# x laid out by features, and 1 / rms(x) moved from the rows of x to the results of the projections

## The chip, the cores and the metric

The kernel runs on one core of a Trainium2 chip. A core has a matrix engine, TensorE (PE in the profile; PEld is its loading of weights), VectorE (DVE), ScalarE (ACT), GpSimd (POOL) and SyncE (SP), which here only issues transfers (DMAs). Each engine executes its own list of instructions in order and waits on semaphores for the others. The metric is the device time of one execution in microseconds (us); of several runs the median counts.

## What is computed

One layer of a streaming encoder on 1024 prompt frames and 64 sample frames of width 1024, 1088 rows in all:

```python
h = rmsnorm(x, g_mix)                       # x * rsqrt(mean(x*x) + eps) * g_mix
[q_a,k_a,v_a | q_b,k_b,v_b | f_b | gate] = h @ w_in
A = band attention(q_a, k_a, v_a)           # 8 heads, QK norm, learned bias
B = forgetting attention(q_b, k_b, v_b)     # 8 heads, c = cumsum of log sigmoid(f + b_f)
x = x + (sigmoid(gate_a) * (A @ w_pa) + sigmoid(gate_b) * (B @ w_pb)) @ w_o
x = x + HierMoE(rmsnorm(x))                 # 32 experts, top-1 group, then top-2 in it
```

Since 1 / rms(x) is one number for each frame, `(x / rms) @ W` equals `(x @ W) / rms`; g_mix is multiplied into the rows of w_in.

## The kernel before

All products that must be exact to fp32 are made of three faster ones: an operand is split into a rounded high part and the rest (`w` hi and lo, `hTh` and `hTl`), and hi*hi, hi*lo and lo*hi are summed in PSUM. Frames stand in nine tiles, eight of 128 prompt frames and tile 8 of the 64 sample frames, taken in the order `TILES` = 0, 1, 2, 3, 4, 5, 8, 6, 7.

`load_x` starts the program: it loads x by frames (128 frames by 1024 features, 512 KB a tile), a few constants, and the weights of the first pair of heads. A frame tile is scaled by 1 / rms (`norm_first` for tile 0, `norm_h` for the others: a square with sum on ACT, two small steps on DVE and POOL, then a multiply of 128x1024 on DVE) and turned: `turn_h` makes eight transposes on PE (L95, 128x128 each), four to a PSUM buffer; ACT copies them to `hTh` (L193) and DVE writes the rest to `hTl` (L194).

`qkv(x)` projects q, k and v of one of eight pairs of heads, x = 0 to 3 of branch A and 4 to 7 of branch B: for every frame tile 24 matmuls of 384 columns (392 for the pair that also carries the forget gates; 16 for tile 8, whose high and low parts stand side by side in one operand). Only `qkv(0)` has the transposes of the next tile between its matmuls, and it is the one that works up all nine frame tiles. ACT copies the result to `raw` (L380), `normalize` and `normalize2` make the QK norm on ACT, DVE and POOL, and `turn_qk` transposes q and k. In the last tile of a pair the weights of the next are split (`load_hi` on ACT, L227; `load_lo` on DVE, L234).

`attention` runs pair by pair, its steps put between the matmuls of later projections, and after the last pair between those of the gates: `gate(ab, c, dst)` computes one of 2 x 8 blocks of 128 gate columns in three slices of 384, 384 and 320 frames, and ACT writes tanh(z / 2) of each to SBUF straight from PSUM (L751). When the prompt's attention of branch B has ended, `swap(1)` frees its memory and starts `sample` for the eight pairs of the sample frames, one every 24 steps. `merge(0)`, the other gates of branch B, and `merge(1)` follow, then `out` (w_o, router) and the experts.

PE's order is the program's order, written with two counters (`at`: steps, one for three matmuls; `late`: modelled PE time). For the other engines and SP a scheduler orders the instructions from a modelled time line, except in the first stage (`self.first`), in which ACT and DVE follow the program too.

## Time and profile before

| | us |
|---|---|
| median of 3 runs (lowest 1236.16, highest 1239.33) | 1238.21 |
| the profiled execution | 1233.42 |
| its span, from the first to the last instruction | 1231.6 |
| PE busy in the span | 1175.8 |
| DVE, ACT, POOL busy | 800.6, 740.5, 317.7 |

The profiled execution is 1.82 us longer than its span and 4.79 us below the median. PE is busy almost throughout: the three stretches with less are the first 10 us, the sample frames' attention around 610 to 700 us, and the experts at the end, where the DMA engines are near full.

### The profile page before, as it was taken

To read this page: it belongs to the slowest core of one execution; us is meant where nothing else is said; L and a number is where in the kernel's file an instruction comes from. 1 tells how busy PE (TensorE), PEld (TensorE's weight loads), DVE (VectorE), ACT (ScalarE), POOL (GpSimd) and SP (SyncE) were. 2 spreads that over 40 slices of the span, in tenths; PEclk is the share of its full clock that TensorE was granted. 3 is DMA by queue.
4 is the path that set the end of the run, shared out by engine and by line. 5 is a ranking of instruction groups with operands and counts; after the bars stand their busy time and mean duration, and the time that the engine had idled before them with its cause. 6 is when DMAs were issued, how large, how long until landed. Compare 5 with 4: busy or idle time off the path is not lost. (4 is left out here: it accounts for less than half of the span.)

```text
span 1231.6 us, 22308 instructions
## 1 busy us (share of the span) xinstructions
PE 1175.8 (95%) x7605; PEld 1098.2 (89%) x7605; DVE 800.6 (65%) x2476; ACT 740.5 (60%) x1730; POOL 317.7 (26%) x469
## 2 busy tenths in 40 slices
PE   8999999999999999999999899999999979999983
PEld 6899999999889999899899899999988859999972
DVE  6768776767498897978467686218644444665553
ACT  5789998989498898988566344323233322333321
POOL 2643435353433444100000000000000013455421
PEclk9999999999999999999999999999999998999998
DMA  8112121222323140411234332214574458999994
GB/s 285 53 58 88 37 73 53 67 70 66 74 70 69 51 87 30 83 56 40 66 94 120 100 92 84 80 45 129 205 282 167 154 191 258 282 280 263 269 276 112
DMA packets 102539, 152.65 MB, mean 124 GB/s; under 512 B 14477, under 2 KB 78837, under 8 KB 102389
## 3 DMA queue, kind: packets, MB, share of 16 engines
q1 hardware_dynamic: 92789, 124.43, 33.6%
q0 software_dynamic: 7168, 17.84, 6.4%
q10 hardware_dynamic: 2464, 8.91, 1.8%
q8 instruction: 61, 1.00, 0.3%
q14 instruction: 57, 0.47, 0.1%
HBM read 122.08 MB, written 38.23 MB: 130 GB/s over the span
## 5 line engine op out<-in xcount | busy, mean ns | idle before, releaser
L83 PE MATMUL big<-w,hTh 128*128 128x384 f32 (+1 forms) x1152 | 322.9, 351 | 1.1 <-ACT raw L380 0.4
L83 PEld LDWEIGHTS big<-w,hTh 128*128 128x128 f32 x1152 | 203.9, 189 | 6.5 <-ACT w L227 1.1
L83 PE MATMUL big<-hTh,w 128*128 128x384 f32 (+1 forms) x768 | 204.0, 334 | 0.0
L83 PE MATMUL big<-w,hTl 128*128 128x384 f32 (+1 forms) x512 | 172.9, 338 | 1.3 <-DVE hTl L194 1.3
L83 PEld LDWEIGHTS big<-hTh,w 128*128 128x128 f32 x768 | 137.7, 188 | 1.2
L83 PE MATMUL big<-hTl,w 128*128 128x384 f32 (+1 forms) x384 | 126.0, 328 | 0.0
L636 DVE TENSOR_TENSOR PT<-small,PT 128x512 fp32r<-128x512 f32 (+2 forms) x192 | 98.7, 519 | 16.5 <-ACT PT L635 15.0
L536 ACT ACTIVATE S<-S,mns 128x640 f32<-128x640 f32 (+7 forms) x128 | 94.1, 735 | 23.7 <-DVE mns L598 22.4
L83 PE MATMUL big<-ath,w 128*128 128x384 f32 (+1 forms) x384 | 99.4, 335 | 0.0
L540 ACT ACTIVATE S<-S,rc 128x640 f32<-128x640 f32 (+7 forms) x128 | 93.8, 736 | 8.2 <-DVE rc L538 7.3
L83 PEld LDWEIGHTS big<-w,hTl 128*128 128x128 f32 x512 | 96.6, 189 | 1.8 <-DVE hTl L194 1.6
L95 PE MATMUL small<-ident,S 128*128 128x128 f32 x528 | 89.4, 274 | 3.4 <-ACT S L540 2.9
L635 ACT CAST PT<-small 128x512 fp32r<-128x512 f32 (+2 forms) x192 | 84.5, 447 | 11.2 <-PE small L83 4.7
L83 PE MATMUL small<-PT,v 128*128 128x256 f32 x608 | 83.6, 283 | 0.0
L83 PEld LDWEIGHTS small<-PT,v 128*128 128x128 f32 x608 | 79.5, 189 | 0.5 <-DVE PT L636 0.2
L411 POOL TENSOR_TENSOR ssr<-ssa,mhalf 128x8 f32<-128x8 f32 (+1 forms) x40 | 61.2, 1530 | 69.2 <-DVE ssa L410 58.4
L95 PEld LDWEIGHTS small<-ident,S 128*128 128x128 f32 x528 | 66.2, 140 | 11.5 <-ACT S L540 5.0
L83 PE MATMUL big<-wo,mh 128*128 128x512 f32 x288 | 75.9, 402 | 0.0
L83 PEld LDWEIGHTS big<-hTl,w 128*128 128x128 f32 x384 | 72.4, 189 | 0.1
L83 PEld LDWEIGHTS big<-ath,w 128*128 128x128 f32 x384 | 69.0, 190 | 1.4
L83 PE MATMUL big<-k,qh 128*128 128x320 f32 (+3 forms) x192 | 65.2, 343 | 4.7 <-DVE mns L598 4.4
L449 POOL TENSOR_TENSOR v<-raw,v 128x128 fp32r<-128x128 f32 x64 | 33.3, 521 | 134.5 <-DVE v L448 127.6
(259 smaller groups left out, 2554.9 us busy)
## 6 DMA issues: line engine op xcount, KB each, us to landing
uo<-in_w SPq DMA_DIRECT2D x43, 512.0 KB, 8.2
ux<-in_w SPq DMA_DIRECT2D x30, 512.0 KB, 7.6
ur<-in_w SPq DMA_DIRECT2D x23, 512.0 KB, 7.6
wraw<-in_w_pair SPq DMA_DIRECT2D x56, 192.0 KB, 2.8
wraw<-in_w_in SPq DMA_DIRECT2D x32, 192.0 KB, 2.5
atd<-at SPq DMA_DIRECT2D x32, 128.0 KB, 1.7
bias<-ccd SPq DMA_DIRECT2D x8, 512.0 KB, 9.1
y<-in_x_prompt SPq DMA_DIRECT2D x8, 512.0 KB, 4.3
```

What stands on the lines that cost most here:

```text
L83: self.nc.tensor.matmul(out, a, b, start=start, stop=stop)
L95: self.nc.tensor.transpose(out, a, ident)
L411: nc.gpsimd.tensor_tensor(r[:n, :4 * c], a[:n, :4 * c], self.mhalf[:n, :4 * c], op=OP.pow)
L449: (nc.gpsimd if V_POOL & 2 else nc.vector).tensor_tensor(V[:, i, :, 64:128], src, V[:, i, :, 0:64].bitcast(F32), op=OP.subtract)
L536: nc.scalar.activation(S[:nq, :n], S[:nq, :n], AF.Exp, bias=mn[:nq], scale=-1.0, accum_out=sm[:nq])
L540: nc.scalar.activation(S[:nq, :n], S[:nq, :n], AF.Copy, scale=rc[:nq])
L635: nc.scalar.copy(hi, pt[:, sr, :])
L636: nc.vector.tensor_tensor(PT[:, 1, sr, 128 * j:128 * j + 128], pt[:, sr, :], hi.bitcast(F32), op=OP.subtract)
```

## The change

x comes in laid out by features as well (`x_t`, `x_ts`, made on the host), so that the transposes go: `split_x` copies a whole tile of 128 features x 8 x 128 frames to `hTh` on ACT and subtracts on DVE. x by frames is still loaded, behind it, for the sum of squares alone (`norm_x`); 1 / rms stands in `self.r`, one column for a tile. The copies from PSUM to `raw` multiply by it. For the gates it is needed along the frames: it goes out to DRAM with the transposed `cc`, and in `swap(1)` one DMA brings it to all 128 partitions (`rb`, 128x1088). Gate results are copied plainly from PSUM; `squash` then multiplies by `rb` on POOL and takes tanh on ACT. Slices that were done before `swap(1)` wait in `bare`. Before the sample's memory is freed, `keep_r` copies `rb` to three of the four small PSUM buffers, and the later gates of branch B multiply on DVE from there. Some sample buffers (`qh`, `sat`, `sbot`) go from two to one, the two copies of cached rows (`rolled`) are asked for 60 steps later, and the warm-up matmuls use `tribig` in place of the removed `identb`.

```diff
     def load_x(self):
-        self.xs = [self.xp.tile([128, D], F32, name=f"x{i}") for i in range(NT)]
-        for hf in range(2):
-            sl = slice(512 * hf, 512 * hf + 512)
-            nc.sync.dma_start(self.xs[0][:, sl], self.x_rows(0)[:, sl])
+        self.xt[0] = self.xp.tile([128, 8, 128], F32, name="xt", bufs=5)
+        nc.sync.dma_start(self.xt[0][:, 0:2], I["x_t"][0][:, 0:2])
         self.late_consts()
-        self.norm_first()
...
+        self.load_hi(0, 0)
+        nc.sync.dma_start(self.xt[0][:, 2:4], I["x_t"][0][:, 2:4])
+        self.split_x(0, 0, 2)
+        self.load_lo(0, 0)
+        self.load_hi(0, 1)
+        self.split_x(0, 2, 4)
+        self.load_lo(0, 1)
...
+        nc.sync.dma_start(self.xt[0][:, 4:8], I["x_t"][0][:, 4:8])
+        self.split_x(0, 4, 8)
...
+        for o, i in enumerate(TILES):
+            if o:
+                self.xt[i] = self.xp.tile([128, 8, 128], F32, name="xt", bufs=5)[:, :, :rows(i)]
+                nc.sync.dma_start(self.xt[i], I["x_t"][i] if i < 8 else I["x_ts"])
+            if o:
+                self.load_rows(TILES[o - 1])
...
+    def split_x(self, i, k0, k1):
+        nc, n = self.nc, rows(i)
+        h, l = (x[:, k0:k1, 128 * i:128 * i + n] for x in (self.hTh, self.hTl))
+        x = self.xt[i][:, k0:k1]
+        nc.scalar.copy(h, x)
+        nc.vector.tensor_tensor(l, x, h.bitcast(F32), op=OP.subtract)
...
+    def norm_x(self, i):
+        nc, x = self.nc, self.xs[i]
+        jk = self.xp.tile([128, D], BF, name="jk")
+        ss = self.sp.tile([128, 1], F32, name="ssx")
+        nc.scalar.activation(jk, x, AF.Square, accum_out=ss)
+        nc.vector.tensor_scalar(ss, ss, 1.0 / D, EPS, op0=OP.mult, op1=OP.add)
+        nc.gpsimd.tensor_tensor(self.r[:, i:i + 1], ss, self.mhalf[:, 0:1], op=OP.pow)
...
     def qkv(self, x):
-                    self.at(H_TURN, self.turn_h, TILES[o + 1], 0)
-                    self.at(H_TURN + 1, self.turn_h, TILES[o + 1], 4)
...
+            if x == 0 and 0 < o < NT - 1:
+                self.split_x(TILES[o + 1], 0, 8)
+            if x == 0 and o:
+                self.norm_x(i)
...
-                nc.scalar.copy(raw[:, i % 2], ps[:, :384])
+                nc.scalar.activation(raw[:, i % 2], ps[:, :384], AF.Copy, scale=self.r[:, i:i + 1])
...
     def gate(self, ab, c, dst):
-            nc.scalar.activation(dst[:, s0:s0 + sn], ps[:, :sn], AF.Tanh, scale=0.5)
+            nc.scalar.copy(dst[:, s0:s0 + sn], ps[:, :sn])
+            if self.rb:
+                self.squash(dst, s0, sn)
+            else:
+                self.bare.append((dst, s0, sn))
+    def squash(self, dst, s0, sn):
+        nc, d = self.nc, dst[:, s0:s0 + sn]
+        if len(self.rb) == 3:
+            nc.vector.tensor_tensor(d, d, self.rb[s0 // 384][:, :sn], op=OP.mult)
+        else:
+            nc.gpsimd.tensor_tensor(d, d, self.rb[0][:, s0:s0 + sn], op=OP.mult)
+        nc.scalar.activation(d, d, AF.Tanh, scale=0.5)
+    def load_r(self, pool):
+        rb = pool.tile([128, NTOK], F32, name="rb", bufs=1)
+        self.nc.sync.dma_start(rb, self.rd.partition_broadcast(128))
+        self.rb = [rb]
+    def keep_r(self):
+        ps = [self.pp.tile([128, 384], F32, name="small", bufs=NSMALL) for _ in SL]
+        for (s0, sn), x in zip(SL, ps):
+            self.nc.scalar.copy(x[:, :sn], self.rb[0][:, s0:s0 + sn])
+        self.rb = ps
...
         def swap(br):
-            for x, pr in enumerate(pairs):
+            self.sample(*pairs[0])
+            self.load_r(self.sm_)
+            for y, x in enumerate(self.bare):
+                self.at(4 + 2 * y, self.squash, *x)
+            for x, pr in enumerate(pairs[1:], 1):
                 self.at(1 + S_EVERY * x, self.sample, *pr)
```

On PE the transposes of x leave `qkv(0)`; nothing else of PE's order moves by more than a few matmuls. At the start of the program, the last matmuls of tile 0, before (`x1` is tile 1 by frames, turned for the next round):

```order
L83 MATMUL big_230<-w_172,hTh_91 128x384
L95 MATMUL small_242<-ident_72,x1_125 128x128 x4
L83 MATMUL big_230<-w_174,hTh_91 128x384
L83 MATMUL big_230<-w_200,hTh_91 128x384
L83 MATMUL big_230<-w_200,hTl_92 128x384
L95 MATMUL small_252<-ident_72,x1_125 128x128 x4
L83 MATMUL big_230<-w_206,hTh_91 128x384
```

and the same place in the changed kernel, all eight features' blocks of tile 0:

```order
L84 MATMUL big_229<-w_151,hTh_89 128x384
L84 MATMUL big_229<-w_157,hTh_89 128x384
L84 MATMUL big_229<-w_164,hTh_89 128x384
L84 MATMUL big_229<-w_164,hTl_90 128x384
L84 MATMUL big_229<-w_170,hTh_89 128x384
L84 MATMUL big_229<-w_170,hTl_90 128x384
```

The two groups of four transposes are gone, and matmul follows matmul.

On ACT, at the change from pair 0 to pair 1 (`jk` is the square of a frame tile, `w<-wraw` a split of pair 1's weights, `qh<-q` the first of eight copies for the attention), before:

```order
L183 ACTIVATE jk_647,ssx_648<-x7_131 128x1024
L382 COPY raw_627<-big_567 64x384
L405 ACTIVATE sq_630<-raw_627 64x256
L193 CAST hTh_91<-small_664 128x4x128
L193 CAST hTh_91<-small_674 128x4x128
L503 CAST qh_836<-q_469 64x256
```

and after:

```order
L406 ACTIVATE sq_524<-raw_521 64x256
L184 CAST hTh_89<-xt_215 128x8x128
L194 ACTIVATE jk_534,ssx_535<-x_217 128x1024
L227 ACTIVATE w_595<-wraw_593,small_124 128x392
L194 ACTIVATE jk_572,ssx_573<-x_219 128x1024
L227 ACTIVATE w_601<-wraw_599,small_124 128x392
L504 CAST qh_716<-q_417 64x256
```

The eight copies to `qh` stand behind two squares and two splits of weights that wait for PE; the other splits of pair 1 follow them, as before.

On ACT, in the first steps of the sample frames (`sk`: keys of a sample pair, `sS`: its scores, `m`: a gate slice), before:

```order
L504 CAST qh_8783<-sqk_8781 64x64
L483 CAST sk0_8872<-sqk_8781 64x64
L536 ACTIVATE sS_8707,sm_8717<-sS_8707,mns_8708 64x576
L751 ACTIVATE m_8613<-big_8668 128x384
L212 ACTIVATE w_8635<-wraw_8634,small_135 128x128 x2
L212 ACTIVATE w_8808<-wraw_8807,small_135 128x128 x3
L483 CAST sk1_8873<-sqk_8781 64x64
```

and after:

```order
L484 CAST sk1_8804<-sqk_8704 64x64
L765 ACTIVATE m_7427<-m_7427 128x384
L723 CAST sPT_8693<-small_8687 128x4x64
L212 ACTIVATE w_8733<-wraw_8732,small_124 128x128 x3
L752 COPY m_8498<-big_8637 128x320
L765 ACTIVATE m_7427<-m_7427 128x320
L537 ACTIVATE sS_8667,sm_8677<-sS_8667,mns_8668 64x576
L765 ACTIVATE m_7699<-m_7699 128x384
```

The tanh of older slices (L765), each of which waits for a multiply on POOL, now stand between the steps of the sample's softmax.

## Rows read from the trace of the kernel before

**Rows 1.** The page: busy time by engine; DMA share in 40 slices.

```profile
PE 1175.8 (95%) x7605; PEld 1098.2 (89%) x7605; DVE 800.6 (65%) x2476; ACT 740.5 (60%) x1730; POOL 317.7 (26%) x469
...
DMA  8112121222323140411234332214574458999994
```

**Rows 2.** PE's waits: line, releaser: us in total, times, longest.

```profile
PE small L95 <- DVE sat L736: 1.9, 1, 1.9
...
PE small L95 <- DVE x L185: 1.3, 2, 1.1
```

**Rows 3.** Time line of the start: start us, us, engine, line, out<-in, count [idle <-releaser].

```profile
3.52 0.63 ACT L168 ACTIVATE jk<-x 128x512 f32<-128x512 f32 x1 [1.52 <-DMA x<-in_x_prompt]
...
5.79 1.12 ACT L227 ACTIVATE w<-wraw,small 128x384 fp32r<-128x384 f32 x2 [1.55 <-DMA wraw<-in_w_pair]
...
7.07 1.12 ACT L227 ACTIVATE w<-wraw,small 128x384 fp32r<-128x384 f32 x2 [0.16 <-DMA wraw<-in_w_pair]
...
8.76 0.45 PE L83 MATMUL big<-w,hTh 128*128 128x384 f32 x1 [0.24 <-ACT hTh L193]
...
10.54 0.45 PE L83 MATMUL big<-w,hTl 128*128 128x384 f32 x1 [1.33 <-DVE hTl L194]
...
16.04 0.48 ACT L380 COPY raw<-big 128x384 f32<-128x384 f32 x1
```

**Rows 4.** Time line of PE in the last tile of qkv(0) and into qkv(1).

```profile
51.43 0.60 PE L95 MATMUL small<-ident,x 128*128 128x128 f32 x4
51.79 0.42 PE L83 MATMUL big<-w,hTh 128*128 128x384 f32 x1
52.05 0.34 PE L83 MATMUL big<-w,hTl 128*128 128x384 f32 x1
...
55.36 0.34 PE L83 MATMUL big<-w,hTh 128*128 128x384 f32 x1
55.53 0.60 PE L95 MATMUL small<-ident,raw 128*128 128x128 f32 x4
55.89 0.60 PE L83 MATMUL big<-w,hTh 128*128 128x384 f32 x2
...
58.43 0.34 PE L83 MATMUL big<-w,hTl 128*128 128x392 f32 x1
```

**Rows 5.** Stretches of 2 us: busy time by engine, PE clock, DMA share, GB/s.

```profile
12.00:14.00 2.00, 1.95 (x15) 1.59 (x14) 2.00 (x4) 1.47 (x3) 0.00 (x0) 1.00 1.04 426
...
18.00:20.00 2.00, 1.98 (x15) 1.97 (x16) 0.69 (x1) 0.94 (x2) 0.00 (x0) 1.00 0.97 324
```

**Rows 6.** Groups by shape: count, busy us, mean ns, idle before.

```profile
L183 ACT ACTIVATE jk<-x 128x1024 f32<-128x1024 f32 x7 | 7.4, 1061 | 0.5 <-DMA x<-in_x_prompt 0.5
...
L1092 DVE TENSOR_TENSOR w2l<-ur,w2h 128x1024 fp32r<-128x1024 f32 x8 | 9.8, 1223 | 6.6 <-ACT w2h L1090 6.6
```

**Rows 7.** Time line of ACT where qkv(1) begins.

```profile
52.55 0.40 ACT L503 CAST qh<-q 64x256 fp32r<-64x256 f32 x1
...
55.96 1.14 ACT L227 ACTIVATE w<-wraw,small 128x392 fp32r<-128x392 f32 x2
...
58.09 1.13 ACT L227 ACTIVATE w<-wraw,small 128x392 fp32r<-128x392 f32 x2
```

**Rows 8.** A 10 us stretch of the sample frames; then groups for prices.

```profile
690.00:700.00 10.00, 6.91 (x35) 6.25 (x34) 6.03 (x21) 3.40 (x12) 0.31 (x1) 0.83 0.45 126
...
L422 POOL TENSOR_TENSOR raw<-raw,ssr 128x256 f32<-128x256 f32 x64 | 40.4, 652 | 2.1
...
L751 ACT ACTIVATE z<-big 128x384 f32<-128x384 f32 x16 | 7.8, 490 | 31.1 <-PE big L83 31.0
```

**Rows 9.** Time lines of POOL and DVE, 55 to 61 us.

```profile
55.42 3.61 POOL L522 TENSOR_SCALAR bias<-bias 128x640 f32<-128x640 f32 x2
...
56.62 1.75 DVE L234 SCALAR_TENSOR_TENSOR w<-wraw,small,w 128x392 fp32r<-128x392 f32 x2 [0.20 <-ACT w L227]
...
59.66 1.16 DVE L234 SCALAR_TENSOR_TENSOR w<-wraw,small,w 128x392 fp32r<-128x392 f32 x2
```

More of the change, by code (lines that the diff above doesn't have):

```diff
@@ L125, in late_consts @@
         self.kg = p.tile([128, 2, 64], F32, name="kg")
+        self.ccr = p.tile([128, 113], F32, name="ccr")
+        self.r = self.ccr[:, 104:113]
     def rstd(self, ss, n, width):
@@ L158, in load_x @@
             self.load_lo(0, k)
-        for i in TILES[2:]:
-            nc.sync.dma_start(self.xs[i][:rows(i)], self.x_rows(i))
-        nc.sync.dma_start(self.kg, I["k_gain"])
-    def norm_first(self):
-        nc, x = self.nc, self.xs[0]
-        jk = self.xp.tile([128, D], F32, name="jk")
-        ss = self.sp.tile([128, 2], F32, name="ss")
-        nc.scalar.activation(jk[:, :512], x[:, :512], AF.Square, accum_out=ss[:, 0:1])
-        nc.vector.tensor_tensor_reduce(out=jk[:, 512:], in0=x[:, 512:], in1=x[:, 512:], scale=1.0, scalar=0.0,
-                                       op0=OP.mult, op1=OP.add, accum_out=ss[:, 1:2])
-        nc.vector.tensor_tensor(ss[:, 0:1], ss[:, 0:1], ss[:, 1:2], op=OP.add)
-        r = self.rstd(ss[:, 0:1], 128, D)
-        for hf in range(2):
-            sl = slice(512 * hf, 512 * hf + 512)
-            nc.vector.tensor_scalar(x[:, sl], x[:, sl], r, None, op0=OP.mult)
@@ L177, in norm_h @@
-    def norm_h(self, i):
-        nc, x, n = self.nc, self.xs[i], rows(i)
-        jk = self.xp.tile([128, D], F32, name="jk")
-        ss = self.sp.tile([128, 1], F32, name="ssx")
-        with self.tc.issue_after(self.turned.ins):
-            nc.scalar.activation(jk[:n], x[:n], AF.Square, accum_out=ss[:n])
-        r = self.rstd(ss, n, D)
-        nc.vector.tensor_scalar(x[:n], x[:n], r[:n], None, op0=OP.mult)
-    def turn_h(self, i, k0):
-        nc, x, n = self.nc, self.xs[i], rows(i)
-        ps = self.pp.tile([128, 4, 128], F32, name="small", bufs=NSMALL)
-        for k in range(4):
-            self.tr(ps[:, k, :n], x[:n, 128 * (k0 + k):128 * (k0 + k) + 128], self.ident[:n, :n])
-        h, l = (x[:, k0:k0 + 4, 128 * i:128 * i + n] for x in (self.hTh, self.hTl))
-        self.turned = nc.scalar.copy(h, ps[:, :, :n])
-        nc.vector.tensor_tensor(l, ps[:, :, :n], h.bitcast(F32), op=OP.subtract)
-        if i == NT - 1:
-            nc.scalar.copy(self.hTh[:, k0:k0 + 4, NTOK:], l)
+        for o, i in enumerate(TILES):
[4 more added lines that the diff above has]
+                self.load_rows(TILES[o - 1])
@@ new lines, in load_x, with load_rows @@
+        self.load_rows(TILES[-1])
+        nc.sync.dma_start(self.kg, I["k_gain"])
+        self.split_x(TILES[1], 0, 8)
+        self.norm_x(TILES[0])
+    def load_rows(self, i):
+        x = self.xs[i] = self.xp.tile([128, D], F32, name="x", bufs=5)
+        for h in range(1 if i < 8 else 2):
+            self.nc.sync.dma_start(x[64 * h:64 * h + rows(i)], self.x_rows(i))
+    def split_x(self, i, k0, k1):
[4 more added lines that the diff above has]
+        nc.vector.tensor_tensor(l, x, h.bitcast(F32), op=OP.subtract)
+        if i == NT - 1:
+            nc.scalar.copy(self.hTh[:, k0:k1, NTOK:], l)
@@ L313, in sums @@
             self.mm(pc[:, 0], self.tri, lff, start=True, stop=True)
[L314 removed]
+            self.mm(pc[:, 1], self.ones.to_broadcast([128, 128]), lff, start=True, stop=True)
             acc = fp.tile([128, 13, 8], F32, name="acc")
@@ L678, in sample2 @@
         self.stack_k([k[:, 512:] for k in ks], qk[:, 1])
-        at = P.tile([128, 64], F32, name="sat")
+        at = P.tile([128, 64], F32, name="sat", bufs=1)
         def head(h):
@@ L732, in values @@
                 self.mm(po, V[:n, i, :], PT[:n, i:i + 2], start=(i == 0), stop=(i == 4))
-            bot = P.tile([64, 128], F32, name="sbot")
+            bot = P.tile([64, 128], F32, name="sbot", bufs=1)
             nc.scalar.copy(bot, po[64:128, :128])
@@ L1273, in run @@
         self.warm(WARM0)
-        self.first = tc.manual_schedule(engines={mybir.EngineType.Activation, mybir.EngineType.DVE})
+        self.first = tc.manual_schedule(engines={mybir.EngineType.Activation, mybir.EngineType.DVE,
+                                                         mybir.EngineType.SP})
         self.first.__enter__()
@@ L1307, in run @@
             self.merge(0, c, self.m[c], at[0])
+        self.keep_r()
         self.close("sm")
```

64 lines of the change are left out of this document (30 added, 34 removed).

## The prediction

> **What bounds the kernel now.** I read the page first: PE is busy for 95% of the span, the other engines for 26 to 65%, and the DMA engines are full only in the first slice and at the end [rows 1]. So PE's own list of instructions is the bound, except where it waits; the reader is to see that work taken off PE counts in full as long as the engines that feed it keep up. The list of PE's waits then says how much it waits at all: single waits of one or two microseconds, among them 1.3 us for the scaled x (two waits) and 1.9 us in the sample frames' attention [rows 2]. Two stretches are touched by the change, and I read their time lines: the start up to qkv(1), and the sample frames' attention from about 604 us on.
>
> At the start PE warms up until 6 us and gets its first useful matmul at 8.76 us, the first with `hTl` at 10.54 us; ACT copies out the result of tile 0 at 16.04 us, so tile 0 ends at 16.0 [rows 3]. Its 24 matmuls alone would take 4.2 us, so about 5 us there are waits for the normalized and turned x, and for weights. From 16.0 us on PE runs tile after tile until qkv(1): its first matmul stands one step of 0.17 us ahead of the row at 58.43, at 58.25 us [rows 4]. That is 42.25 us for eight tiles. A matmul steps on by 0.174 us (from 52.05 to 55.36 there are 19, 3.31 / 19) [rows 4]. Eight tiles have 7 x 24 + 16 = 184 matmuls, 32.0 us. A group of four transposes costs 0.36 us and 0.09 more on the matmul behind it (51.43 to 51.79, then 0.26 instead of 0.17 to 52.05) [rows 4]. The three groups for q and k (one at 55.53) cost 3 x 0.45 = 1.35 us and stay [rows 4]. What is left, 42.25 - 32.0 - 1.35 = 8.9 us, belongs to the transposes of x: sixteen groups at 0.45 us are 7.2, and waits for x the rest [rows 2].
>
> **The change, part by part.** *The start.* The weights and x of tile 0 must now land, be split, and that is all. In the trace, data had landed after 0.262 MB (half of x) by 3.52 us, after 0.73 MB by 5.79, after 1.12 MB by 7.07 [rows 3]; the last two give 0.39 MB in 1.28 us, 0.305 MB/us. The changed kernel needs x of tile 0 (0.52 MB) and eight weights of 0.197 MB, 2.11 MB with the constants: 7.07 + 0.99 / 0.305 = 10.3 us for the last weight. Its split takes 0.56 us on ACT (1.12 for two) [rows 3] and about 0.6 on DVE (1.16 for two) [rows 9], so 11.5 us; with four last matmuls, 0.7 us with rounding up for hand-overs down to 0.5, tile 0 ends at 12.0 instead of 16.0.
>
> Tile 1 comes right behind in the queue: 0.52 MB of 4 KB rows, which x had by frames too and which ran at 426 GB/s [rows 5], so 11.6 us. Its copy to `hTh` is now one instruction of 1024 columns, as the square on ACT, 1.06 us; the subtraction is the same form as the experts' w2l on DVE, 1.22 us [rows 6]. So the second matmul of tile 1 can start at about 14.0 us, and PE stands for 1.8 us. From there: 23 matmuls to 18.0 us, then 160 more, 27.8 us, and 1.35 us for q and k: qkv(1) would begin at 47.2 us instead of 58.25. **Gain 11.0 us.**
>
> Can DMA keep this pace? In the changed order 12.35 MB stand ahead of the last frame tile's end, since x is loaded twice and the two copies of cached rows still stand among the loads. From 11.6 us, 9.7 MB take 23 us at 426 GB/s and 30 us at 324 [rows 5]: landed by 34.4 to 41.5 us, 2.3 us more for the split [rows 6]. The tile is wanted at 47.2 - 4.3 = 42.9. So it is in time at the one and 0.9 us late at the other; at the 0.305 of the first microseconds it would be 2.9 us late. I take 0 and keep 2.9 as the end. The squares and the multiply by 1 / rms on the way to `raw` cost PE nothing: four PSUM buffers of 4.2 us each cover the few microseconds that the copy waits for `r`. The multiply of 128x1024 on DVE goes, which nothing but PE's 1.3 us waited for [rows 2].
>
> *The beginning of qkv(1).* Here ACT becomes late. Before, the eight copies to `qh` ran from 52.55 us, the splits of pair 1's weights followed at 55.96 and 58.09, so the fourth was done at 59.2, 0.95 us after qkv(1) began [rows 7]. In the new order two squares and two splits stand ahead of `qh`, and the second split can't run before PE has let go of a weight buffer in the last tile, which begins at 42.9: first split to 44.0, a square (1.06 and 0.19 for the sum) to 45.3, second split to 45.9, `qh` (3.4 us as before) to 49.3, two splits to 50.5. That is 3.3 us after 47.2, 2.35 later than before, and the static order of PE waits for it. **Loss 2.3 us**, between 0 (the scheduler's order leaves ACT a gap that I don't see) and 3.5 (the later splits slip as well).
>
> *The gates.* Every one of 48 slices gets one more pass of ACT (0.49 us, the form of today's tanh [rows 8]), 23 us spread over 280 us in which ACT is half idle; 30 of them get a multiply of 128x384 on POOL, 18 on DVE. The price of the multiply stands between 0.65 us (128x256, two inputs [rows 8]) and 1.8 us (128x640, one input [rows 9]); by size 0.65 x 384 / 256 = 0.98, nearest to the first. POOL has 0.3 us of work in 10 there [rows 8], so 30 us are free. merge(0) wants the first slices only after all gates of branch A, tens of us later. What is on the path is the sample frames' softmax: ACT is in order, a tanh that waits for POOL holds the exponentials and copies behind it, and PE waits for these with matmuls of gates queued behind. There PE has 3.1 us idle in the worst 10 us, and its granted clock fell to 0.83 after the waits [rows 8]. One or two delays of a tanh's length at the five places where PE waits today make +1.5 us; I keep -2 (the waits and the fall of the clock at 690 us vanish by a shift) to +8 as bounds. `rb` itself, 0.56 MB, goes out behind the first sample pair's loads and delays only the squashes. `keep_r` takes three of four small PSUM buffers, but only after the last sample step and until the gates end, when nothing else asks for them.
>
> *The rest* (the constants, `rolled`, the warm-up's operand, single buffers for `sat` and `sbot`): nothing on PE; the experts' stage starts when PE frees its buffers, so it moves along with PE, DMA-heavy as it is.
>
> **The sum.** -11.0 + 2.3 + 1.5 = -7.2 us. The profiled execution has 1233.42 us, 1.82 more than its span; it would go to 1226.2 (span 1224.4). The median of the runs is 4.79 above it, so the prediction for the median is 1238.21 - 7.2 = 1231.0 us.
>
> **The rivals.** *More comes through* (1226.0 and less): ACT catches up before qkv(1), and DMA goes at 400 from the start, so tile 0 ends at 11. Then -12 to -14 us: 1224.2 to 1226.2. For it: the rate of 426; against: ACT's order [rows 7]. *Feeding eats it:* the loads run at 0.305, so the last tile waits 2.9, qkv(1) loses 3.5, the samples 2: -11.0 + 8.4 = -2.6, 1235.6, within what can be told from no change. For it: x is loaded twice, and the DMA engines are full at 12 to 20 us already [rows 5]; against: the rows of x ran at 426. *POOL and DVE hold each other up, and it gets slower.* While POOL ran its two instructions of 1.8 us from 55.42 on, two splits on DVE took 1.75 us; just after, two took 1.16 [rows 9]. So a DVE instruction lost 0.59 us to a POOL instruction that reads SBUF. Thirty multiplies among the sample's DVE steps, 0.59 each, are 17.7 us; if all of it reached PE, the end would be -8.7 + 17.7 = +9.0, 1247.2 us. It decides from 8.7 / 30 = 0.29 us lost on PE for each multiply. Against it: PE waits only at some five places there, the others have slack, and many of DVE's inputs there come from PSUM.
>
> The Trainium skill has the rule for this in "SBUF — State Buffer", section "Who interferes with whom": a DVE instruction with two SBUF inputs and a GpSimd instruction that reads SBUF contend for a shared port, and whichever starts second waits for the whole of the other. By it each multiply could hold DVE for its full length, 0.98 us by my price, 29 us in all and 1259 us if PE paid everything. The trace shows a delay of that kind, but of 0.59 us in an instruction of 1.8, so I keep the row's number.
>
> That the transposes would not leave PE is excluded: the order of PE shows it.
>
> **How the numbers follow.** A difference of less than 0.3%, 3.7 us, can't be told from no change here. My forecast, a gain of 4 to 12 us, gets 0.62; the larger gain 0.14; feeding 0.17; slower 0.07. So faster 0.76, same 0.17, slower 0.07. The range reaches from the best case, -14, to the feeding case with the samples at +4 instead of 2, -0.6, rounded to 1224 to 1237; the slower case stays out.
>
> **What would show it.** In the changed profile: the first `raw` copy no longer bound to 16 us (tile 0 done near 12); no transposes of x; PE's stall before tile 1 of 1 to 2 us on `hTl`; the first matmul of qkv(1) near 47 us, and waits of PE there for `w`; the stretch from the first matmul of qkv(1) to `swap(1)` as long as before; then squashes of about 1 us on POOL, and PE's waits in the sample stretch at 6 to 10 us. I would be wrong if PE waited for `xt` in the middle of qkv(0), or if the sample stretch grew by more than 5 us; the first would show DMA, the second ACT's or DVE's order.

## The result, and the profile after

The changed kernel takes 1244.03 us (median of five runs, 1243.13 to 1246.41) where the kernel before takes 1238.21 in runs beside it: a ratio of 1.0052, 95% interval 1.0036 to 1.0068. It is slower by 5.8 us; 7.2 us faster was forecast. Its profiled execution has 1243.13 us, with a span of 1241.3, 9.7 more than the span before. The medians are only 5.8 apart because the profiled execution of before was a quick one, 4.79 us below its median, and that of after only 0.9 below.

The page of the changed kernel, busy time by engine (answers [rows 1]):

```profile
PE 1179.0 (95%) x7533; PEld 1098.2 (88%) x7533; DVE 812.7 (65%) x2474; ACT 766.1 (62%) x1771; POOL 346.7 (28%) x499
```

The transposes of x are gone, yet PE is busy for 3.2 us longer than before: part of its work ran at a lower clock. To see where time came and went, take one matmul that stands in both traces and subtract its start before from its start after. PE is ahead by 9.0 us at the first matmul of `qkv(1)` (49.25, one step ahead of the row at 49.43 below, against 58.25), by 6.5 once 70 us are reached, by 5.7 at the first transposes of the sample frames (602.83 against 608.57). Then, at a score of a later sample pair, it is 9.7 behind (709.95 against 700.23), and stays so: 10.0 behind at 760 us, 9.5 at 950. **The whole turn lies in 100 us, the sample frames' stretch: 15.5 us lost there.** This difference, 709.95 - 602.83 less 700.23 - 608.57, is called the stretch's loss below. The four rows, before and then after:

```profile
608.57 0.63 PE L95 MATMUL small<-ident,rk 128*128 128x128 f32 x4 [0.79 <-DMA rk<-in_cache_a_k]
...
700.23 0.35 PE L83 MATMUL big<-sk,qh 128*64 128x288 f32 x1
```

```profile
602.83 0.63 PE L96 MATMUL small<-ident,rk 128*128 128x128 f32 x4 [0.77 <-DMA rk<-in_cache_a_k]
...
709.95 0.35 PE L84 MATMUL big<-sk,qh 128*64 128x288 f32 x1
```

The start, time line of PE in the changed kernel (answers [rows 3] and [rows 4]):

```profile
12.60 0.86 PE L84 MATMUL big<-w,hTh 128*128 128x384 f32 x4
13.83 0.44 PE L84 MATMUL big<-w,hTh 128*128 128x384 f32 x1 [0.37 <-ACT hTh L184]
15.09 0.44 PE L84 MATMUL big<-w,hTl 128*128 128x384 f32 x1 [0.82 <-DVE hTl L185]
...
44.68 0.44 PE L84 MATMUL big<-w,hTl 128*128 128x384 f32 x1 [0.42 <-DVE ssx L195]
...
49.43 0.34 PE L84 MATMUL big<-w,hTl 128*128 128x392 f32 x1
...
51.32 0.45 PE L84 MATMUL big<-w,hTh 128*128 128x392 f32 x1 [0.61 <-ACT w L227]
...
54.13 0.45 PE L84 MATMUL big<-w,hTh 128*128 128x392 f32 x1 [0.57 <-ACT w L227]
```

and of ACT in the same places (answers [rows 7]):

```profile
12.73 1.05 ACT L184 CAST hTh<-xt 128x1024 fp32r<-128x1024 f32 x1 [0.64 <-DMA xt<-in_x_t]
...
45.16 0.62 ACT L227 ACTIVATE w<-wraw,small 128x392 fp32r<-128x392 f32 x1 [1.08 <-PE big L84]
45.69 1.04 ACT L194 ACTIVATE jk<-x 128x1024 bf16<-128x1024 f32 x1
...
50.64 1.14 ACT L227 ACTIVATE w<-wraw,small 128x392 fp32r<-128x392 f32 x2
```

The last matmul of tile 0 begins at 12.60 + 3 x 0.17 = 13.1, the second of tile 1 at 15.09, and from tile 1 on only three waits of 0.4, 0.8 and 0.4 us are left on the way to `qkv(1)`. There the third and fourth split of pair 1's weights come at 50.64, behind the square at 45.69 and the eight copies to `qh`, and PE waits for splits.

Now the sample frames. PE's waits from 600 to 710 us, in us in total, times, longest; first before (the fifth is in [rows 2]), then after:

```profile
PE big L83 <- DVE sk L484: 1.8, 1, 1.8
PE small L83 <- DVE sPT L723: 1.2, 1, 1.2
PE small L95 <- DVE sS L542: 0.8, 1, 0.8
PE small L95 <- DMA rk<-in_cache_a_k: 0.8, 1, 0.8
```

```profile
PE small L84 <- DVE sPT L724: 10.0, 6, 2.6
PE big L84 <- DVE sk L485: 2.2, 1, 2.2
PE small L96 <- DVE sS L543: 1.9, 1, 1.9
PE small L96 <- DMA rk<-in_cache_a_k: 0.8, 1, 0.8
```

With the 1.9 us for `sat`, 6.5 us became 14.9: 8.4 us more; the waits for `sPT`, which DVE writes, alone grew by 8.8. The other part is the clock. Windows (busy us of PE, its weight loads, DVE, ACT, POOL; granted clock; DMA share; GB/s), before:

```profile
600.00:710.00 110.00, 103.41 (x640) 96.54 (x639) 75.02 (x257) 59.81 (x174) 3.44 (x11) 0.98 0.37 105
```

and after, the same stretch and two pieces of it:

```profile
600.00:710.00 110.00, 95.06 (x543) 87.46 (x541) 74.15 (x219) 63.13 (x180) 32.11 (x39) 0.92 0.36 102
...
621.00:625.00 4.00, 0.62 (x3) 0.41 (x3) 3.93 (x7) 1.98 (x7) 3.34 (x4) 1.00 0.18 54
625.00:632.00 7.00, 6.71 (x23) 5.66 (x24) 2.83 (x10) 3.57 (x9) 1.32 (x2) 0.51 0.34 101
```

PE stands almost idle from 621 to 625 us, and in the 7 us behind that the granted clock is 0.51: the level of 1.2 GHz instead of 2.4. Over 110 us the mean fell from 0.98 to 0.92, which is 0.06 x 110 = 6.6 us of matmul time. Waits and clock, 8.4 + 6.6 = 15.0, come near the 15.5.

The first 2.1 of the 15.5 us have another cause than POOL's multiplies, for e1 below, which has none, loses them too: PE's lead falls from 5.7 to 3.6 us between 608 and 616 us of the time before. PE waits 2.2 us for `sk` there instead of 1.8, and behind that wait the granted clock is at half for 3.4 us, from 608.1 us, which the kernel before does not have. The DVE step that wrote this `sk` had its usual length, 0.68 us.

Who is late? POOL, DVE and PE in the changed kernel's time line where most of it is lost:

```profile
607.22 17.12 POOL L764 TENSOR_TENSOR m<-m,rb 128x320 f32<-128x320 f32 x18 [19.36 <-DMA rb<-ccd]
```

```profile
613.85 4.00 DVE L213 SCALAR_TENSOR_TENSOR w<-wraw,small,w 128x128 fp32r<-128x128 f32 x4 [1.74 <-ACT w L212]
...
618.79 1.03 DVE L506 TENSOR_TENSOR ql<-sqk,qh 64x64 fp32r<-64x64 f32 x1
...
620.68 0.92 DVE L485 TENSOR_TENSOR sk<-sqk,sk 64x64 fp32r<-64x64 f32 x1
621.63 0.42 DVE L724 TENSOR_TENSOR sPT<-small,sPT 128x256 fp32r<-128x256 f32 x1
621.97 2.52 DVE L213 SCALAR_TENSOR_TENSOR w<-wraw,small,w 128x128 fp32r<-128x128 f32 x3
```

```profile
622.11 0.62 PE L84 MATMUL small<-sPT,sv 128*128 128x256 f32 x3 [2.06 <-DVE sPT L724]
625.29 1.09 PE L84 MATMUL small<-sPT,sv 128*128 128x256 f32 x2 [2.56 <-DVE sPT L724]
```

POOL runs 18 multiplies without a break, 0.95 us each: `rb` had landed, and 14 older slices had been waiting for it. They were written 2 steps apart (L1320), but POOL's order comes from the scheduler. Meanwhile four splits of weights take 1.00 us each on DVE, and a subtract of 64x64 takes 0.9 to 1.0. The `sPT` that PE waits for stands behind them in DVE's order. Compare what these steps take on average from 603 to 700 us (groups by shape: count, busy us, mean ns, idle before), before:

```profile
L213 DVE SCALAR_TENSOR_TENSOR w<-wraw,small,w 128x128 fp32r<-128x128 f32 x23 | 7.1, 345 | 0.9 <-ACT w L212 0.8
...
L723 DVE TENSOR_TENSOR sPT<-small,sPT 128x256 fp32r<-128x256 f32 x10 | 4.1, 414 | 0.1
...
L505 DVE TENSOR_TENSOR ql<-sqk,qh 64x64 fp32r<-64x64 f32 x14 | 3.0, 217 | 1.2 <-ACT qh L503 1.0
```

and after:

```profile
L213 DVE SCALAR_TENSOR_TENSOR w<-wraw,small,w 128x128 fp32r<-128x128 f32 x18 | 10.5, 627 | 4.1 <-ACT w L212 4.1
...
L506 DVE TENSOR_TENSOR ql<-sqk,qh 64x64 fp32r<-64x64 f32 x12 | 4.1, 345 | 3.3 <-ACT qh L504 3.2
...
L724 DVE TENSOR_TENSOR sPT<-small,sPT 128x256 fp32r<-128x256 f32 x9 | 3.8, 418 | 1.1 <-ACT sPT L723 1.1
```

Steps that read two operands from SBUF (L213, L506) grew by more than half; the one with an operand in PSUM (`small`, L724) did not. Step by step it is plainer: of L213, L506 and the 64x64 subtract of L485, 14 steps between 600 and 705 us begin at least 0.2 us before a multiply ends, and all 14 end 0.08 to 0.15 us behind that end. A DVE step that starts beside a multiply waits for the rest of it.

### The profile page after: what moved, and what is told of

Read it like the earlier page. It is cut to its first block, busy times and chain, and to the rows that moved or that the text cites. A ratio compares the mean times of both kernels' runs of the same rounds, so it can differ in the third digit from the quotient of the medians.

```text
span 1241.3 us, 22272 instructions
## 1 busy us (share of the span) xinstructions
PE 1179.0 (95%) x7533; PEld 1098.2 (88%) x7533; DVE 812.7 (65%) x2474; ACT 766.1 (62%) x1771; POOL 346.7 (28%) x499
## 3 DMA queue, kind: packets, MB, share of 16 engines
q1 hardware_dynamic: 95346, 129.71, 34.2%
## 5 line engine op out<-in xcount | busy, mean ns | idle before, releaser
L84 PE MATMUL big<-hTh,w 128*128 128x384 f32 (+1 forms) x768 | 207.8, 338 | 0.0
L84 PEld LDWEIGHTS big<-hTh,w 128*128 128x128 f32 x768 | 140.7, 192 | 1.4 <-issue 0.2
L637 DVE TENSOR_TENSOR PT<-small,PT 128x512 fp32r<-128x512 f32 (+2 forms) x192 | 98.8, 519 | 16.8 <-ACT PT L636 14.9
L96 PEld LDWEIGHTS small<-ident,S 128*128 128x128 f32 x528 | 65.9, 140 | 13.5 <-ACT S L541 5.8
```

The lines of the kernel that those rows point to most:

```text
L84: self.nc.tensor.matmul(out, a, b, start=start, stop=stop)
L96: self.nc.tensor.transpose(out, a, ident)
L637: nc.vector.tensor_tensor(PT[:, 1, sr, 128 * j:128 * j + 128], pt[:, sr, :], hi.bitcast(F32), op=OP.subtract)
```

## The experiments

Theory *port*: POOL's multiplies hold DVE's steps, so DVE hands its results to PE late. Rivals: the second pass of every gate slice through ACT; the shift or the single buffers; DVE's load as such. The table has all runs; the edits are against the changed kernel. "Ahead" is PE's lead on before at the sample's first transposes, "loss" the stretch's loss (both from the trace of one execution of each run); the clock is the granted one from 600 to 710 us.

| run | ratio to before (95%) | ahead | loss | clock |
|---|---|---|---|---|
| the change | 1.0052 (1.0036 to 1.0068) | 5.7 | 15.5 | 0.92 |
| e4_gates_plain | 0.9947 (0.9929 to 0.9964) | 4.8 | -0.8 | 0.98 |
| e1_no_mult | 0.9980 (0.9964 to 0.9995) | 5.3 | 4.5 | 0.95 |
| e2_no_tanh | 1.0036 (1.0017 to 1.0056) | 6.7 | 13.5 | 0.91 |
| e6_pool_alone | 1.0030 (1.0013 to 1.0048) | 4.4 | 8.8 | 0.95 |
| e17_pool_writes | 0.9987 (0.9968 to 1.0007) | 6.4 | 4.5 | 0.95 |
| e3_mult_dve | 1.0066 (1.0049 to 1.0083) | 4.5 | 14.6 | 0.91 |
| e5_spread | 1.0084 (1.0055 to 1.0113) | 5.6 | 14.8 | 0.92 |
| e8_spread_dve | 1.0094 (1.0061 to 1.0127) | 6.3 | 15.4 | 0.91 |
| e7_fused_spread | 1.0047 (1.0027 to 1.0066) | 6.4 | 14.1 | 0.91 |
| e9_queued | 1.0031 (1.0019 to 1.0043) | 4.8 | 8.9 | 0.97 |
| e10_late | 1.0045 (1.0026 to 1.0063) | 6.6 | 4.7, and 8.4 behind it | 0.95 |
| e12_late_qh | 1.0053 (1.0033 to 1.0072) | 6.0 | 5.3, and 8.9 behind it | 0.95 |
| e14_even | 1.0021 (1.0007 to 1.0035) | 5.6 | 7.7 | 0.95 |
| e15_even_qh | 1.0028 (1.0013 to 1.0042) | 7.5 | 7.9 | 0.95 |
| e16_late_rb | 1.0040 (1.0024 to 1.0055) | 5.9 | 9.8 | 0.94 |

Where the gates lack their factor (e1, e2, e4, e6, e17), frames go to other experts, and the experts' stage differs by a few us: e4 gained 3.4 us between 950 and 1030 us and had lost it again by 1200; e1 and e6 lost 4.3 and 6.9 us behind 1150. The loss, which lies ahead of the experts, is the number to compare. Pairs of kernels whose order in the stretch is nearly the same (the change and e5, e3 and e8, e10 and e12, e14 and e15) differ in it by 0.2 to 0.8 us, which tells how much the loss from one trace is worth.

**Which part of the change.**

```diff
# e4_gates_plain: in gate(), no rb, no squash, no keep_r
-            nc.scalar.copy(dst[:, s0:s0 + sn], ps[:, :sn])
...
+            nc.scalar.activation(dst[:, s0:s0 + sn], ps[:, :sn], AF.Tanh, scale=0.5)
# e1_no_mult: in squash()
-        else:
-            nc.gpsimd.tensor_tensor(d, d, self.rb[0][:, s0:s0 + sn], op=OP.mult)
# e2_no_tanh: in squash(), behind POOL's multiply
+            return
```

> Only the start of the program is changed: the gates take tanh straight from PSUM as in the kernel before, without 1 / rms (left out: the factor on the gates, rb and the copies of it). It tells what the start alone brings. From the trace of the changed kernel, PE is 6.5 us ahead of before at 65 us and 5.2 ahead at 604. If the whole loss lies in the gates' part, the sample stretch loses 1 us or less and the time is 1238.2 - 5.5 = 1232.7. If the stretch still loses 5 us or more, the loss comes from the shift or from the single buffers for qh, sat and sbot, and the time is 1238 or more.

> Leaves out the 30 multiplies by 1 / rms on POOL (L764), so the gates of these slices are those of the unscaled x; the extra tanh pass on ACT, the copies from PSUM and rb stay. Theory port: in the changed kernel DVE's small steps on SBUF operands wait for POOL's multiplies (18 of them stand back to back from 607 to 624 us, and subtracts of 64x64 that take 0.22 us elsewhere take up to 1.03 there), so the sample steps come late and PE waits. By it the sample stretch (from the first sample transposes at 602.8 us to 700) loses 3 us or less against before instead of 15.3, the subtracts are back at 0.22, and the time is about 1244 - 12 = 1232. Rival ACT: the 30 tanh passes (0.5 us each) hold up the copies and exponentials of the sample in ACT's order. By it the stretch still loses 10 or more, and the time stays above 1240.

> Leaves out the tanh of the 30 slices that POOL multiplies (L765 there), so these gates enter the merge without tanh; the multiplies on POOL stay. Theory port: the sample stretch still loses 10 us or more against before, the first sPT of the low part comes late on DVE as in the changed kernel, and the time stays at 1240 or above. Rival ACT: the stretch loses 3 us or less, the time falls to about 1232. A loss halfway (6 to 8 us) would say that both have a part.

With the gates plain the stretch loses nothing (-0.8), and the kernel is 0.5% faster than before: the start brings PE to the sample frames 4.8 us ahead, and the shift and the single buffers cost nothing. Without the multiplies the loss falls from 15.5 to 4.5; without the tanh only to 13.5. So the multiplies make 11 of the 15.5 us, and the rival ACT is a small part, not the cause. e1 had been expected at a loss of 3 or less. Its 4.5 are not the second pass on ACT alone: 2.1 of them lie between 608 and 616 us as in the changed kernel, and e1 has the transfer of `rb`, which e4 lacks.

**How POOL's multiply holds DVE.** In e6 nobody waits for POOL; in e17 POOL works as many times but reads nothing.

```diff
-            nc.gpsimd.tensor_tensor(d, d, self.rb[0][:, s0:s0 + sn], op=OP.mult)
# e6_pool_alone
+            b = self.rb[0][:, s0:s0 + sn]
+            nc.gpsimd.tensor_tensor(b, b, self.ones.to_broadcast([128, sn]), op=OP.mult)
# e17_pool_writes
+            nc.gpsimd.memset(self.rb[0][:, 0:832], 1.0)
```

> As the run without POOL's multiplies, but POOL multiplies the same stretch of rb by ones in their place, in rb itself: 30 instructions on POOL, in SBUF, on which no engine waits (left out: the factor on the 30 slices). The tanh passes wait for nothing new. Theory port: DVE's steps with two operands in SBUF are stretched although nothing depends on POOL: the weight splits (L213) go from a mean of 344 to over 450 ns, the 64x64 subtracts from 220 to over 300, and the stretch loses 5 us or more beyond the 4.5 of the run without multiplies. Rival dependence: what cost time was that tanh, and all behind it on ACT, waited for POOL's result. Then DVE's means stay at 344 and 220 and the time is that of the run without multiplies, 0.998 of before.

> As the run in which POOL multiplied rb by ones and nobody waited for it, but POOL only writes: each of the 30 multiplies is a memset of 128x832 in rb, about 1 us by the 0.31 us of a memset of 128x256 (left out: the factor on the gates). POOL is as busy and its queue as long, but it reads nothing. Theory port: what holds DVE is POOL's reading of SBUF; the Trainium skill (SBUF — State Buffer, section Who interferes with whom) says that an instruction of POOL that only writes does not contend with a DVE instruction of two SBUF inputs. By it the weight splits (L213) stay at 344 ns and the 64x64 subtracts at 220, the stretch loses 4 to 5 us as in the run without multiplies, and the time is 0.996 to 1.000 of before. Rival queue: POOL's being busy holds up the memsets of sPT behind it in its order, and so PE; then L213 stays at 344 but the stretch loses 7 or more. Rival any use: L213 rises to 450 or more as in the run with reads.

The same groups on DVE, 603 to 700 us, in e6:

```profile
L213 DVE SCALAR_TENSOR_TENSOR w<-wraw,small,w 128x128 fp32r<-128x128 f32 x18 | 8.4, 514 | 2.1 <-ACT w L212 2.1
...
L506 DVE TENSOR_TENSOR ql<-sqk,qh 64x64 fp32r<-64x64 f32 x12 | 3.4, 283 | 2.7 <-ACT qh L504 2.6
```

in e1 (no multiplies):

```profile
L213 DVE SCALAR_TENSOR_TENSOR w<-wraw,small,w 128x128 fp32r<-128x128 f32 x18 | 5.5, 344 | 4.6 <-ACT w L212 4.6
...
L506 DVE TENSOR_TENSOR ql<-sqk,qh 64x64 fp32r<-64x64 f32 x12 | 2.6, 217 | 2.4 <-ACT qh L504 2.4
```

and in e17, with POOL's own group below:

```profile
L213 DVE SCALAR_TENSOR_TENSOR w<-wraw,small,w 128x128 fp32r<-128x128 f32 x18 | 5.4, 343 | 4.0 <-ACT w L212 4.0
...
L688 DVE CAST sv<-rv 64x64 fp32r<-64x64 f32 x11 | 4.0, 364 | 0.1
...
L506 DVE TENSOR_TENSOR ql<-sqk,qh 64x64 fp32r<-64x64 f32 x12 | 2.6, 217 | 2.2 <-ACT qh L504 2.2
```

```profile
L764 POOL MEMSET rb<- 128x832 f32 x30 | 24.9, 831 | 19.9 <-DMA rb<-ccd 18.4
```

In e6 the splits on DVE are at 514 ns although nothing depends on POOL, and the loss is 8.8, 4.3 more than without (its POOL instructions are shorter, 0.78 us in the first row of 17, and since they wait for `rb` alone the last ends before 638 us; how much of the other 6.7 us that explains is open. ACT waiting for POOL is not most of it: e2, in which no tanh waits for a multiply, lost 13.5). In e17 POOL is busy for 24.9 us in 30 instructions, all between 606 and 638 us as well, the splits are at 343, ten that begin beside a memset take 0.33 to 0.35 us each, and the loss is 4.5, that of e1. So it is POOL's reading of SBUF that holds DVE, neither its queue nor its being busy. The Trainium skill states it in "SBUF — State Buffer", section "Who interferes with whom": a DVE instruction with two SBUF inputs contends with a GpSimd instruction that reads SBUF, not with one that only writes. The three traces agree, with 514, 344 and 343 ns.

**Close together or one by one, on POOL or on DVE.** Four runs only moved the multiplies as written:

```diff
# e3_mult_dve: in squash();  e8: this and the line of e5;  e7: e8, and new slices are
# multiplied by DVE straight from PSUM, in place of ACT's copy
-            nc.gpsimd.tensor_tensor(d, d, self.rb[0][:, s0:s0 + sn], op=OP.mult)
+            nc.vector.tensor_tensor(d, d, self.rb[0][:, s0:s0 + sn], op=OP.mult)
# e5_spread: in swap()
-                self.at(4 + 2 * y, self.squash, *x)
+                self.at(4 + 8 * y, self.squash, *x)
```

> The 30 multiplies of 128x384 and 128x320 move from POOL to DVE; nothing is left out. Theory port: DVE takes them at some 0.5 us each, 15 us over 100 us in which it is 60 to 70% busy, and no longer waits for POOL; the sample stretch loses 2 to 6 us against before instead of 15.3, and the time is 1231 to 1237. Rival ACT: the stretch loses as much as now, 1242 or more. Rival DVE load: 18 multiplies in a row hold up DVE's own order as much as POOL did, 1240 or more.

> The 14 squashes of slices that were done before swap(1) are put 8 steps (4.2 us) apart instead of 2 (1.04 us, as long as one multiply on POOL takes); POOL still multiplies. Theory port: each multiply can still hold one or two DVE steps, by up to 0.8 us, but DVE has time to catch up in between, and POOL is no longer busy without a break from 607 to 624 us; the sample stretch, which loses 15.3 us against before in the changed kernel, loses 4 to 8, and the time is 1238 minus 5 plus that, 1237 to 1241. If the number of multiplies counts and not their closeness, the loss stays at 12 or more and the time above 1243.

> As the run with all 30 multiplies on DVE, which lost 7.5 us between 616 and 620 us where its 14 older slices stood in a row, but with these 8 steps apart; ACT still copies from PSUM first. If the row was the cause, that loss goes and the stretch loses 2 to 6 us, 1234 to 1239; the difference to the fused run is what 16 copies on ACT cost. If DVE's load as such is the cause, 1242 and above.

> POOL has no multiply any more. For the 16 slices that PE finishes between swap(1) and the end of the sample frames, DVE multiplies by rb straight from PSUM, in place of ACT's copy; the 14 older ones are multiplied by DVE in SBUF, 8 steps apart. Nothing is left out. Theory port: DVE gets 30 x 0.5 us, spread, ACT loses 16 copies, no step waits for POOL; the sample stretch loses 0 to 4 us against before, and the time is 1231 to 1236, below the kernel before by up to 0.5%. Rival (passes on ACT and DVE's load cost this, wherever they stand): the stretch loses 7 or more, 1240 and above.

All four lost 14 to 15 us, against what I expected of each. Time lines tell why: in e5 POOL's row of multiplies stands where it stood (first fence), and in e3 DVE takes the 14 older slices in a row (second fence):

```profile
606.91 17.16 POOL L764 TENSOR_TENSOR m<-m,rb 128x320 f32<-128x320 f32 x18 [18.80 <-DMA rb<-ccd]
```

```profile
608.70 6.32 DVE L764 TENSOR_TENSOR m<-m,rb 128x320 f32<-128x320 f32 x14
615.05 0.69 DVE L485 TENSOR_TENSOR sk<-small,sk 64x512 fp32r<-64x512 f32 x1
```

The step at which a multiply is written does not place it; the scheduler issues it as soon as `rb` is there. So e5, e7 and e8 are no tests of spreading. e3 does say that without POOL a row of multiplies on DVE costs as much: the key at 615.05 (`sk`), whose high part ACT had done at 609.03, waited 6.0 us behind them. To spread them in fact, e9 and e14 queue each older slice behind an instruction of its engine:

```diff
# e9_queued: in gate(); no loop over bare in swap()
-                self.squash(dst, s0, sn)
+                p = self.squash(dst, s0, sn)
+                if self.bare:
+                    with self.tc.issue_after(p):
+                        self.squash(*self.bare.pop(0))
# e14_even: on DVE; new slices of branch A straight from PSUM; older ones behind the latest
# score step of the sample; the six slices z of branch B among the later gates
+            if self.rb and len(self.rb) == 1:
+                self.behind(self.dv, self.bare)
# e10_late: on DVE; all slices of A ahead of their merge
+            p = nc.vector.scalar_tensor_tensor(zz, zz, 1.0, ps[:, :sn], op0=OP.add, op1=OP.mult)
+            if ab == 0 and c < 7:
+                self.behind(p.ins)
```

> The run with the 14 older squashes 8 steps apart had POOL's multiplies at the same places as the changed kernel (18 in a row from 607 us): the scheduler issues them as soon as rb is there, whatever step they are written at. Here each of the 14 is queued on POOL behind the multiply of a newer slice, so they come one by one, some 5.5 us apart, and end near 685 us; POOL still multiplies all 30. Theory closeness: the row of 18 was the harm, since DVE had no time to catch up; the sample stretch loses 3 to 8 us against before instead of 15.3, and the time is 1235 to 1240. Rival number: each multiply costs PE what it costs DVE (30 x 0.3 to 0.5 us), wherever it stands; the stretch loses 10 or more and the time stays above 1241.

> Nothing is left out. No multiply on POOL; slices of branch A that PE finishes among the sample frames are multiplied by DVE straight from PSUM (no copy on ACT), the 14 older ones are queued on DVE one by one behind the sample's score steps, and the six early slices of branch B are copied plainly and multiplied among the later gates. So the sample's stretch gets 24 multiplies of 0.5 us on DVE, one or two to each head, and none in a row. Theory closeness (a row of multiplies, on POOL or DVE, makes DVE late and PE waits; single ones are absorbed): the stretch 608 to 700 loses 1 to 5 us against before (8.9 when POOL's were queued one by one, 15.3 in the changed kernel), PE waits there 6 to 9 us, one or two stretches at the half clock, and the time is 0.996 to 1.000 of before. Rival total work: 24 x 0.55 us of DVE cost what they cost in the other runs with DVE (13 to 14 us); the time is 1.004 or more.

> All 30 multiplies and their tanh leave the sample frames' stretch: DVE multiplies each slice of branch A three slices ahead of its merge (queued behind the splits of A for the first three, behind the merge's own steps for the others), and the six slices of branch B in the later gates. Nothing is left out. Theory: what costs time is work put on DVE, ACT or POOL among the sample's steps, and nothing else; then the stretch 608 to 690 loses no more than 1 us as in the run with plain gates, the merges lose 0 to 3 us more, and the time is 1228 to 1232, faster than before by 0.3 to 0.7%. Rival: the work only moves its cost, merge(0) becomes bound by DVE and loses 8 or more, 1236 and above.

POOL in e9, whose multiplies now stand in pairs, behind a first row of four:

```profile
608.28 3.77 POOL L767 TENSOR_TENSOR m<-m,rb 128x320 f32<-128x320 f32 x4 [19.31 <-ACT sk L484]
613.66 1.85 POOL L767 TENSOR_TENSOR m<-m,rb 128x384 f32<-128x384 f32 x2 [1.61 <-ACT m L752]
620.05 1.83 POOL L767 TENSOR_TENSOR m<-m,rb 128x320 f32<-128x320 f32 x2 [4.53 <-ACT m L752]
```

The same 30 multiplies on POOL cost 8.9 us instead of 15.5, somewhat above the 3 to 8 expected; on DVE, 24 of them spread cost 7.7 instead of 14 to 15, where 1 to 5 were expected. So closeness makes 6.6 of the 11.0 us that the multiplies on POOL cost, and the multiplies as such the other 4.4; e1's 4.5 lie beside that. On DVE the share of the work as such was not measured apart, since e14 also moves six multiplies out of the stretch. e10 shows from another side that the work has its price: with the work moved out, the stretch loses 4.7, but the merges behind it, beside which the last sample pairs still run, lose 8.4 between 700 and 760 us. The rival "the work only moves its cost" was right there.

**The beginning of qkv(1), and rb's transfer.**

```diff
# e12_late_qh (e10 and this), e15_even_qh (e14 and this): in scores(); self.hi is the last split on ACT
-            G["q"] = self.stack_q(self.ap_, q, 256)
+            with self.tc.issue_after(self.hi.ins) if (br, p, g) == (0, 0, 1) else nullcontext():
+                G["q"] = self.stack_q(self.ap_, q, 256)
# e16_late_rb: e15, in swap(); and two older slices at a time while more than eight are left
-            self.load_r(self.sm_)
+            self.at(22, self.load_r, self.sm_)
```

> As the run with the late multiplies, and in addition the second half of the eight copies to qh is queued on ACT behind the last split of pair 1's weights. If the 2.3 us that PE lost at the beginning of qkv(1) came from ACT's order (squares, splits, eight copies of 0.4 us), this brings 1.0 to 2.0 us there: PE is 7.5 to 8.5 us ahead of before at 65 us instead of 5.5 to 7, and the time is 1 to 2 us below that run. If DVE's splits or the fall of the clock set it, the difference is under 0.5 us.

> As the run before it, with the second half of the copies to qh behind the last split of pair 1's weights, which brought PE from 6.8 to 9.0 us ahead at 62 us, and gave 4 us back at 505 us where POOL's order had come out otherwise. If that second place was an accident of the order, this run is 1 to 2.5 us faster than the one without; if a gain at the start is lost at the next tight place anyway, it is the same within 0.5.

> As the run with even multiplies and late copies to qh (1.0028), but rb is asked for 22 steps (11.5 us) after the first sample pair's loads, so that its 0.56 MB do not run beside them, and the first multiplies come behind the second pair of score steps. Nothing is left out. If the 2.3 us that all kernels with rb lose between 605 and 616 us (and the one with plain gates does not) come from rb's transfer and the multiplies ahead of the first scores, PE loses under 1 us there and the run is 1 to 2.5 us faster than that one: 0.999 to 1.002 of before. If the work is only moved on and lost at the next tight place, it stays at 1.002 to 1.004.

With four of the eight copies to `qh` out of the way, PE is 8.9 and 9.1 us ahead at 70 us (e12, e15) instead of 7.2 and 6.8 (e10, e14), and the stretch at half clock near 55 us is gone: ACT's order at the start of `qkv(1)` did cost those 2 us. But 2 to 4 of them were given back near 505 us, in both runs, where PE waited 1.8 us for `raw` from POOL; by time, neither run differs from the one without the edit beyond their intervals. e16 lost nothing from 608 to 616 us, where e15 lost 2.4. But it is no test of `rb`'s transfer: SP asked for `rb` at 602.22, 1.2 us behind `sqk` where e15 has 0.6, and not the 11.5 us later that the edit meant. What moved are the multiplies, which begin at 615.0 instead of 606.5; yet e1 lost 2.1 us there with no multiply at all, and e3, which asks for `rb` as the changed kernel does, lost nothing. So the cause of those 2 us is open. e16 lost more later (9.8 in all). In both cases the gain went at the next tight place.

No version with the whole computation was faster than the kernel before; e14 comes nearest, at 1.0021.

## Why the prediction was wrong

Point by point, in the order of its steps:

- **Tile 0** was to end at 12.0; its last matmul begins at 13.1. Both the last weight of tile 0 (its split began at 11.47, right when it had landed; 10.3 forecast) and tile 1 of x (12.73; 11.6 forecast) landed 1.1 us late, so the second matmul of tile 1 came at 15.09 instead of 14.0. From there to `qkv(1)` it took 34.2 us instead of 33.2. The gain at that point was 9.0 us, not 11.0: right in kind, two microseconds too large, one by DMA. The last frame tile was 0.4 us late, between 0 and the bound of 2.9, but not by DMA: it had landed at 38.6, and ACT copied it only at 42.01.
- **The beginning of qkv(1)** was to lose 2.3 us; PE's lead fell from 9.0 to 6.5. The place and the size were right, and e12 and e15 confirm the cause, ACT's order. What I did not have is that part of it is paid in clock: the granted clock was at half for 3.4 us from 55.1.
- **From there to the sample frames** nothing was to change; 0.8 us of the lead went in all: 0.5 by 510 us, 1.2 from there to 530, and 1.0 came back. e4 lost the same 1.2 there, so it is not the gates; the cause is open.
- **The sample frames** were to lose 1.5 us, -2 to +8. They lost 15.5. **This is the step that failed**: "one or two delays of a tanh's length at the five places where PE waits today", and nothing for what a multiply on POOL does to DVE. The price of a multiply was right (1.04 us measured for 128x384, 0.98 forecast), and POOL did have the time. Three things in the step were wrong. It spread 30 multiplies evenly over 100 us in mind; the trace has 18 in a row, and spreading them (e9) gave 6.6 us back. It let only ACT's queue pass a delay on to PE; e2, in which no tanh waits for POOL, lost 13.5, so DVE passed it on, held by POOL's reading of SBUF (e6 against e17). And it left the clock out: 0.06 of 110 us, 6.6 us, nearly as much as the waits. Of the 15.5 us the multiplies make 11.0 (e1); of the other 4.5, 2.1 are the wait for the first `sk` and the half clock behind it, and the rest is shared out by no run.
- **The rival "POOL and DVE hold each other up"** came true in kind: it had said 1247.2 us, and 1244.0 were measured. That the totals come so near is in part luck: its sum was -8.7 + 17.7, the traces have -5.7 + 15.5, and the multiplies are 11.0 of that. It had a chance of 0.07, for two reasons that fell. "The others have slack": single steps had, but not a chain of steps each 0.7 us late. "DVE inputs come from PSUM": those were spared, as the 418 ns of L724 show, but they stand in the same order behind those that were not. Its price of 0.59 us for each multiply is what two splits lost together beside two instructions of POOL [rows 9]; singly, the first took its usual 0.62 us (56.62 to 57.24) and the second 1.21. Here a split of weights lost 1.00 - 0.34 = 0.66 us each time in a row and a 64x64 subtract up to 1.03 - 0.22 = 0.8: a DVE step took as long as the multiply it met. On PE 30 multiplies cost (15.5 - 4.5) / 30 = 0.37 us each, above the 0.29 from which that rival decides. The rule of the Trainium skill that the prediction set aside for its row's number ("SBUF — State Buffer", section "Who interferes with whom"), that the second waits for the whole of the other, was right about the 14 steps beside multiplies, though not about the first split of [rows 9].
- **keep_r, the later gates, the merges** cost nothing, as forecast: 9.7 us behind at 700, 10.0 at 760, 9.5 at 950.

So the sum was -11.0 + 2.3 + 1.5; the traces have -9.0 + 2.5 + 0.8 + 15.5, less 0.1 over the rest: +9.7 in the spans.

What stays open: e14 still loses 7.7 us in the stretch with no multiply on POOL and none in a long row. What e1 and e17 lose without such multiplies (4.5, the second passes through ACT and the first wait for `sk` together) and 24 steps of 0.55 us on DVE are in it, but how they divide was not measured.

## What to carry to other kernels

Before a small piece of work is called free because its engine has time, look at what else it holds: here each multiply on POOL held the DVE step with two operands in SBUF that met it until it ended, and the steps of a long dependent chain stood behind it. Look in the order of the engine, not in the code, for how many of them come in a row when the buffer they all wait for arrives. And where PE is the bound, price a wait for itself and for the slow clock that may follow it: here 8.4 us more of waits came with 6.6 us of clock, in e9 5.3 us more with 1.1.
